# The first block's modulation vector made in two halves of the channels instead of whole

## The chip, the cores and the metric

The kernel runs on one core of one Trainium2 chip. The metric is the device time of one execution in microseconds (us). TensorE (PE in the profile) multiplies, with its weight loads listed apart as PEld; VectorE is DVE, ScalarE is ACT, GpSimd is POOL. SyncE (SP) issues nearly all transfers, and the issuing instructions of a queue stand in the profile as SPq or ACTq. All engines run their own instructions in a fixed order and wait for each other by semaphores.

## What is computed

256 tokens of width 1024 pass through two blocks. Only the head of the first one is touched:

```python
def first_block(x, c, ctx, c_ctx, w_ada, b_ada, norm1_g, w_in, ...):
    mod = silu(c) @ w_ada + b_ada                       # 6 x 1024: shift, scale, gate, shift, scale, gate
    sh_a, sc_a, gt_a, sh_m, sc_m, gt_m = split(mod, 6)
    mod_c = silu(c_ctx) @ w_ada + b_ada                 # the same for the context tokens
    csh_a, csc_a, ... = split(mod_c, 6)
    hc = rmsnorm(ctx, norm1_g) * (1 + csc_a) + csh_a
    s_f, s_b = context_states(hc, w_in, w_decay, b_decay)     # k, v and decay of the context
    h = rmsnorm(x, norm1_g) * (1 + sc_a) + sh_a
    x = x + gt_a * token_mixer(h, w_in, ..., s_f, s_b)        # gated linear attention, pool mixer, w_out
    x = x + gt_m * hier_moe(rmsnorm(x, norm2_g) * (1 + sc_m) + sh_m, ...)   # 32 experts, all run
    return rmsnorm(x, final_norm_g)
def reference(...):
    return second_block(first_block(...), ...)          # FFN, attention and retention, FFN, gate
```

So nothing can be multiplied by w_in before the shift and the scale (the first 2048 columns of `w_ada`, 8 MB) are there for the channels in question.

## The kernel before

Weights stream from memory through five buffers of 1 MB (`raw`), filled in turn by SP's queue; a load waits until the buffer's last reader is done, and all that stands behind it on SP waits with it. A large product is made in fp32r with a split: `split` writes the upper part `hi` of a weight piece on ACT (L197) and the rest `lo` on DVE (L198), and each K block (128 channels) takes three matmuls, hi by high part, hi by low part, lo by high part (L293 to L295). The order of instructions on the engines is set by a tile scheduler that goes by the code's order and the data's readiness; `after(...)` and the list `behind` push one instruction of an engine behind others, and `manual_schedule` keeps PE to the order of the code.

The head of the program runs as follows. The first 2048 columns of `w_ada` come as eight loads of 128 x 2048, one for each K block (three, then ctx and x, then five). The silu of c and c_ctx is made from a transposed copy of both vectors (L273, L277), and `ada_row` (L384) multiplies it with each of the eight blocks, four matmuls a block, into one bank. `ada_end` adds the bias (L390) and copies the row (L392); four transposes (L454) turn it, L456 to L460 make the scale (`gaT`), and L467 modulates the transposed and normalized tokens: first the eight blocks of the context `cT`, then the eight of `xT`. Each four blocks are split at once (L197, L198) into `cTh`/`cTl` and the parts of `xT2`. Meanwhile ctx and x are normalized (L426) and transposed (L432).

Then PE computes `aT` (L508, 32 matmuls, the low-rank decay input), the decay product (L521, four fp32 matmuls with `wd`), the panel `pq` (w_in columns 0 to 511: q and k, 48 matmuls of 256 columns for the context and 48 of 512 for x) and the panel `pv` (columns 512 to 1023, 96 matmuls of 512). ACT makes the log of the decay behind L521: Abs into `lt` (L522), a table load, Exp (L526), a table load, Ln (L529); DVE subtracts (L530) and the result is split into `lh`/`ll`. DVE also takes 24 partial products of later `w_ada` columns (`ada_step`, L405). Behind `pv` come the cumulated sums (L543), `ek` (L584, L585), the states (L592), the rest of the mixer, `w_out`, the router (L1039 and after) and the experts, whose first product is L1089. Expert weights come in pieces of 3 MB (`mw`, L703).

Of the kernel before, what the change touches and what calls it, by code (L numbers as in the profile page):

```python
# [81 lines left out]
def body(ctx: ExitStack, tc: tile.TileContext, I, out, dbg=None):  # L82
# [193 lines left out]
    G.memset(sT, 0.0)  # L276
    S.activation(sT[:, :, 0:2], vT[:, 0:16].rearrange("p (v k) -> p k v", v=2), AF.Silu)  # L277
    g1T = vT[:, 16:24]
    pscT = vT[:, 24:28]
    rgnT = vT[:, 28:36]  # L280

    def tok_mm(pa, lhs, w, c0, n, starts, stops, kh, skip=(0, 0)):

        raw = kxn(w, 4 * kh, 4, c0, n)
        for k2 in range(2):
            hi, lo = split(raw[:, 2 * k2:2 * k2 + 2, :])
# [99 lines left out]
    def ada_end(pa, j0, nch):  # L386

        for j in range(nch):
            sel = ident[:12, j0 + j:j0 + j + 1].to_broadcast([12, 32])
            mm(pa[32 * j:32 * j + 32, :], sel, b12, start=False, stop=True)  # L390
# [1314 lines left out]
```

## Time and profile before

| what | value |
|---|---|
| runs of before | 1088.04, 1092.1 and 1092.26 us, median 1092.1 |
| profiled execution | 1089.5 us, span 1087.2 |
| PE busy | 997.5 us (92% of the span), 5785 matmuls |
| PE weight loads | 741.5 us (68%) |
| DVE busy | 648.6 us (60%) |
| ACT busy | 493.5 us (45%) |
| POOL busy | 5.7 us (1%) |
| moved from memory | 258.54 MB, mean 240 GB/s over the span |
| mean granted clock of PE | 0.971 of full speed |

The table says where the engines are over the whole span. A change in the first 60 us is read from that stretch alone: what PE waits for there, and which queue is behind. The rows do that, in the section below.

### The profile page before, as it was taken

Reading aid. Unit: us, or ns where it says so; the run is one execution under the profiler, and the core shown is the slowest. Engines: PE = TensorE matmul, PEld = TensorE weight load, DVE = VectorE, ACT = ScalarE, POOL = GpSimd, SP = SyncE. Lnnn points to the kernel's source line nnn. Section 1 sums busy time; section 2 is a strip of 40 time slices with the busy share of each in tenths; the row PEclk is TensorE's granted clock in tenths of the full one; section 3 lists DMA queues with packets and bytes.
Section 4 is the critical chain, followed back from the end, with each engine's and each line's share of the span. In section 5 each row is a group of like instructions: output and inputs, shape, how many; then the busy total and the mean of one; then the engine's idle time right before and its main releaser. Section 6 shows DMA issues by size and latency. Waiting matters only on the chain.

```text
span 1087.2 us, 15196 instructions
## 1 busy us (share of the span) xinstructions
PE 997.5 (92%) x5785; PEld 741.5 (68%) x5786; DVE 648.6 (60%) x1260; ACT 493.5 (45%) x875; POOL 5.7 (1%) x14
## 2 busy tenths in 40 slices
PE   4799999898878787999999999999999999999996
PEld 1586776343333232888888876787888888888885
DVE  3893865332112124977674499858659677665466
ACT  3534354232112112655553354765565455554353
POOL 1000000000000000000000000000000000000000
PEclk9899998899889999899999999999999999999998
DMA  9786866799989999665555542354367366555511
GB/s 377 275 293 190 305 235 251 293 422 419 422 361 420 422 420 370 211 207 183 205 213 192 157 165 97 130 189 155 117 205 260 120 213 200 173 215 210 187 68 39
DMA packets 114658, 260.59 MB, mean 240 GB/s; under 512 B 7205, under 2 KB 73993, under 8 KB 101273
## 3 DMA queue, kind: packets, MB, share of 16 engines
q1 hardware_dynamic: 114096, 259.31, 65.4%
q8 instruction: 48, 0.79, 0.3%
q10 hardware_dynamic: 488, 0.28, 0.1%
q14 instruction: 26, 0.21, 0.0%
HBM read 258.54 MB, written 1.05 MB: 239 GB/s over the span
## 4 chain that ended last, share of the span: by engine, by line
PE 58%; DMA 6%; DVE 4%; ACT 2%; issue 1%; SPq 0%; DVEq 0%; ACTq 0%
PE mm L311 20%; PE mm L313 9%; PE acc L333 4%; PE acc L335 4%; PE acc L331 4%; DMA mw<-in_w_expert_out_dram 3%; DMA mw<-in_w_expert_in_dram 2%; PE mm L1089 2%; PE acc L1253 2%; PE acc L1252 2%; PE acc L1260 2%; PE acc L294 1%; PE acc L295 1%; PE acc L293 1%; DMA raw<-in_ffn_w_up_dram 1%
## 5 line engine op out<-in xcount | busy, mean ns | idle before, releaser
L198 DVE TENSOR_TENSOR lo<-raw,hi 128x1024 fp32r<-128x1024 f32 (+1 forms) x240 | 287.3, 1205 | 160.6 <-ACT hi L197 158.9
L197 ACT CAST hi<-raw 128x1024 fp32r<-128x1024 f32 (+1 forms) x240 | 246.8, 1036 | 221.1 <-PE mm L311 93.7
L311 PE MATMUL mm<-xT,hi 128*128 128x512 f32 x832 | 211.8, 396 | 0.6 <-DVE rs L1532 0.6
L311 PEld LDWEIGHTS mm<-xT,hi 128*128 128x128 f32 x832 | 148.5, 188 | 28.6 <-DVE rs L1532 1.0
L313 PEld LDWEIGHTS mm<-xT,lo 128*128 128x128 f32 x832 | 110.5, 188 | 9.4
L313 PE MATMUL mm<-xT,lo 128*128 128x256 f32 x832 | 112.1, 277 | 0.0
L1089 PE MATMUL mm<-mw,xg 128*32 (+1 forms) x704 | 85.8, 632 | 11.9 <-DMA mw<-in_w_expert_in_dram 10.9
L1089 PEld LDWEIGHTS mm<-mw,xg 128*32 128x32 f32 x704 | 22.2, 115 | 63.7 <-issue 52.4
L295 PE MATMUL acc<-lo,xT 128*128 128x512 f32 x144 | 57.1, 401 | 1.9 <-DVE lo L198 1.9
L293 PE MATMUL acc<-hi,xT 128*128 128x512 f32 x144 | 58.1, 404 | 0.0
L294 PE MATMUL acc<-hi,xT 128*128 128x512 f32 x144 | 57.7, 401 | 0.0
L335 PE MATMUL acc<-lo,hh 128*128 128x512 f32 x176 | 56.2, 393 | 0.0
L333 PE MATMUL acc<-hi,hl 128*128 128x512 f32 x176 | 56.0, 392 | 0.0
L331 PE MATMUL acc<-hi,hh 128*128 128x512 f32 x176 | 55.9, 392 | 0.0
L1053 ACT ACTIVATE xg<-mm,shT,gmT 128x256 f32<-128x256 f32 (+1 forms) x48 | 23.4, 545 | 67.8 <-PE mm L1039 67.8
L1111 PE MATMUL mm<-mw,z 128*32 128x512 f32 (+1 forms) x352 | 41.5, 601 | 5.5 <-DMA mw<-in_w_expert_out_dram 4.9
L1094 ACT ACTIVATE esg<-mm 128x256 f32<-128x256 f32 x11 | 4.2, 383 | 81.6 <-PE mm L1089 81.6
L1064 DVE TENSOR_TENSOR g<-mm,cst 128x8 f32<-128x8 f32 x11 | 1.8, 167 | 64.5 <-PE mm L1061 64.5
L1252 PE MATMUL acc<-hi,xT 128*128 128x256 f32 (+1 forms) x120 | 37.2, 334 | 2.3 <-ACT xT L197 2.3
L333 PEld LDWEIGHTS acc<-hi,hl 128*128 128x128 f32 x176 | 33.1, 188 | 7.4
L335 PEld LDWEIGHTS acc<-lo,hh 128*128 128x128 f32 x176 | 33.1, 188 | 7.3
L331 PEld LDWEIGHTS acc<-hi,hh 128*128 128x128 f32 x176 | 32.9, 188 | 7.5
(484 smaller groups left out, 1523.6 us busy)
## 6 DMA issues: line engine op xcount, KB each, us to landing
mw<-in_w_expert_in_dram SPq DMA_DIRECT2D x20, 3072.0 KB, 24.8
raw<-in_w_in_dram SPq DMA_DIRECT2D x32, 1024.0 KB, 5.0
mw<-in_w_expert_out_dram SPq DMA_DIRECT2D x10, 3072.0 KB, 26.1
raw<-in_w_ada_dram SPq DMA_DIRECT2D x24, 1024.0 KB, 7.8
raw<-in_ffn_w_gate_dram SPq DMA_DIRECT2D x22, 1024.0 KB, 6.7
raw<-in_ffn_w_up_dram SPq DMA_DIRECT2D x22, 1024.0 KB, 5.4
raw<-in_ffn_w_down_dram SPq DMA_DIRECT2D x22, 1024.0 KB, 5.0
raw<-in_w_out_dram SPq DMA_DIRECT2D x8, 1024.0 KB, 5.0
```

The costliest lines, as they stand in the source:

```text
L197: S.copy(hi, src)
L198: return V.tensor_tensor(lo, src, hi.bitcast(F32), op=ALU.subtract)
L293: mm(o, h_[k][:, c], hi[:, kk, z], start=k == starts, stop=False)
L294: mm(o, l_[k][:, c], hi[:, kk, z], start=False, stop=False)
L295: mm(o, h_[k][:, c], lo[:, kk, z], start=False, stop=k == stops)
L311: mm(pb, hi[:, k, :], x2[k], start=k == 0, stop=False, skip_group_check=True)
L313: mm(pb[:, 0:256], lo[:, k, :], x2[k][:, 0:256], start=False, stop=k == nk - 1, skip_group_check=True)
L331: mm(pa[t][n], hh[k][:, c], hi[:, 0, n * 512:(n + 1) * 512], start=k == seq[0], stop=False)
L333: mm(pa[t][n], hl[k][:, c], hi[:, 0, n * 512:(n + 1) * 512], start=False, stop=False)
L335: mm(pa[t][n], hh[k][:, c], lo[:, 0, n * 512:(n + 1) * 512], start=False, stop=k == seq[-1])
L1089: mm(st_["hp"][32 * i:32 * i + 32, :], xgs[q // 2][k // 4][:, k % 4, c:c + 32], w, start=k == 0, stop=k == KD - 1, skip_group_check=True)
L1252: mm(outs[i][t][:, c], xTh[:, k, tk], hi, start=k == 0, stop=False)
```

## The change

The modulation is made for channels 0 to 511 first and for 512 to 1023 behind it. `ada_half(b, k2)` loads, for half b, two K blocks of the shift's 512 columns and two of the scale's, as two transfers of 128 x 2 x 512 (512 KB with rows of 2 KB) into one `raw` buffer. The channels of c are dealt to partitions as (p k), so c and c_ctx are loaded as columns (`csil`) with no transpose ahead of the silu, and the bias row is loaded on ACT's queue. SP's order is now: one piece of half 0, ctx, one piece, x, two pieces, the first four K blocks of w_in, then all of half 1, then the other four K blocks of w_in.

Half 0 takes 16 matmuls and two for the bias; the row copy is followed by four small matmuls with a selector (`msel`) instead of four transposes. x is transposed behind the last matmul of half 0 (`after([last])`). Then DVE modulates four blocks of the context and four of x, and the panel `pq` starts on K blocks 0 to 3, in two pieces (`k2s`, `parts`). Between the pieces PE makes half 1's 18 matmuls, under `manual_schedule`; the second piece of the context covers the row copy, that of x the small matmuls' outcome. `wah` is split behind the second modulation, `aT` is next to K blocks 4 to 7 of `pq`, and the decay product (L569 now) stands behind the whole panel. `tri` is rounded on ACT (L560) instead of DVE.

```diff
-    nc.scalar.dma_start(vrow[0:8, :], I["c"][0].rearrange("(k p) -> k p", p=P))
-    nc.scalar.dma_start(vrow[8:16, :], I["c_ctx"].rearrange("(k p) -> k p", p=P))
+    csil = small(16, "csil", 1).rearrange("p (v k) -> p v k", v=2)
+    for v, name in enumerate((I["c"][0], I["c_ctx"])):
+        nc.scalar.dma_start(csil[:, v, :], name.rearrange("(p k) -> p k", k=KD))
...
+    G.memset(sT, 0.0)
+    S.activation(sT[:, :, 0:2], csil.rearrange("p v k -> p k v"), AF.Silu)
     ps = bank()
-    nc.tensor.transpose(ps[:, :36], vrow, ident[:36, :36])
-    V.tensor_copy(vT, ps[:, :36])
...
+    def tok_mm(pa, lhs, raw, n, starts, stops, kh, skip=(0, 0), k2s=(0, 1), parts=None):
+        for k2 in k2s:
+            hi, lo = parts or split(raw[:, 2 * k2:2 * k2 + 2, :])
...
-    w_ada0 = [kxn(I["w_ada"][0], k, 1, 0, 2048) for k in range(3)]
...
+    w_in = I["w_in"][0]
+    w_ada = I["w_ada"][0].rearrange("(p k) f -> p k f", k=KD)
...
+    def ada_half(b, k2):
+        w = weight("raw").rearrange("p (j k f) -> p j k f", j=2, k=2)
+        for j in range(2):
+            nc.sync.dma_start(w[:, j], w_ada[:, 2 * k2:2 * k2 + 2, D * j + 512 * b:D * j + 512 * b + 512])
+        return w
+    halves_a = [ada_half(0, 0)]
...
+    halves_a.append(ada_half(0, 1))
...
-    def ada_row(pa, w, k, nch):
-        for j in range(nch):
-            mm(pa[32 * j:32 * j + 32, :], sT[:, k, :], w[:, 512 * j:512 * j + 512], start=k == 0, stop=False)
...
+    halves_a += [ada_half(0, 2), ada_half(0, 3)]
+    first = kxn(w_in, 0, 4, 0, 512)
...
+    msel = small(4, "msel", 1).rearrange("p (j v) -> p j v", j=2)
+    pairs = ident.rearrange("p (e j v) -> p e j v", e=2, j=2)[:, :, :, 0:2]
+    V.tensor_tensor(msel, pairs[:, 0], pairs[:, 1], op=ALU.add)
...
+    def ada_part(pa, w, k2, b):
+        for j in range(2 if k2 == 3 else 0):
+            sel = ident[:12, 2 * j + b:2 * j + b + 1].to_broadcast([12, 32])
+            mm(pa[32 * j:32 * j + 32, :], sel, b12, start=False, stop=False, skip_group_check=True)
+        for kk in range(2):
+            for j in range(2):
+                i = 2 * kk + j
+                last = mm(pa[32 * i:32 * i + 32, :], sT[:, 2 * k2 + kk, :], w[:, j, kk, :], start=k2 == 0,
+                          stop=k2 == 3 and kk == 1, skip_group_check=True)
+        return last
...
+    def ada_row(pa):
         row = t2("modrow")
-        S.copy(row[:32 * nch, :], pa[:32 * nch, :])
-        return row
+        return row, S.copy(row, pa)
...
+    def ada_end(row, b):
+        pt = bank()
+        for s in range(4):
+            mm(pt[:, 4 * s:4 * s + 4], row[:, s * P:(s + 1) * P], msel.rearrange("p j v -> p (j v)"), start=True, stop=True)
+        V.tensor_copy(modT[b], pt[:, 0:16].rearrange("p (s j v) -> p s j v", s=4, j=2))
+        V.scalar_tensor_tensor(gaT[b], modT[b][:, :, 1, :], 1.0, g1T[:, 4 * b:4 * b + 4, None].to_broadcast([P, 4, 2]),
+                               op0=ALU.add, op1=ALU.mult)
...
-    cT, cTt = norm_T(cin, "cT")
-    xT, xTt = norm_T([xres[:, 0, :], xres[:, 1, :]], "xT")
-    pa = acc()
-    for k in range(KD):
-        w = w_ada0.pop(0) if w_ada0 else kxn(I["w_ada"][0], k, 1, 0, 2048)
-        ada_row(pa, w[:, 0, :], k, 4)
-    row = ada_end(pa, 0, 4)
...
+    cT, cTt = turned(normed(cin), "cT")
+    xn = normed([xres[:, 0, :], xres[:, 1, :]])
...
+    def modulate(b, v, src, tiles, hs, ls):
+        for s in range(4):
+            k = 4 * b + s
+            V.tensor_scalar(src[k], src[k], gaT[b][:, s, v:v + 1], modT[b][:, s, 0, v:v + 1], op0=ALU.mult, op1=ALU.add)
+        return split_act(hs[b], ls[b], tiles[b])
...
+    pa = bank()
+    for k2 in range(4):
+        last = ada_part(pa, halves_a[k2], k2, 0)
+    with after([last]):
+        xT, xTt = turned(xn, "xT")
+    row, copied = ada_row(pa)
+    ada_end(row, 0)
+    c_in = (1, cT, cTt, cTht, cTlt)
+    x_in = (0, xT, xTt, [xTh[:, 0:4, :], xTh[:, 4:8, :]], [xTl[:, 0:4, :], xTl[:, 4:8, :]])
+    behind[:] = [copied, modulate(0, *c_in)]
+    nc.sync.dma_start(wa, w_in[:, 1536:1568].rearrange("(k p) f -> p k f", p=P))
+    halves_b = [ada_half(1, k2) for k2 in range(4)]
+    first = [first, kxn(w_in, 4, 4, 0, 512)]
...
-    tri0 = weight("raw")[:, 0:640]
-    nc.sync.dma_start(tri0, I["cst"][:, 512:])
-    V.tensor_copy(tri, tri0)
-    pt = bank()
-    for s in range(4):
-        nc.tensor.transpose(pt[:, s * P:(s + 1) * P], row[:, s * P:(s + 1) * P], ident)
...
-    gaT = cp.tile([P, KD, 2], F32, name="gaT")
-    V.tensor_scalar(gaT, modT[:, 8:16, :], 1.0, None, op0=ALU.add)
-    V.tensor_tensor(gaT, gaT, g1T[:, :, None].to_broadcast([P, KD, 2]), op=ALU.mult)
...
+    pq = [(acc(), acc()), (acc(), acc())]
+    pa = bank()
+    parts = split(first[0][:, 0:2, :])
+    behind[:] = [modulate(0, *x_in)]
+    tok_mm(pq, (cL, xL), first[0], 512, 0, KD - 1, 0, (256, 0), (0,), parts)
+    parts = split(first[0][:, 2:4, :])
+    with tc.manual_schedule(engines={mybir.EngineType.PE}):
+        for k2 in range(4):
+            ada_part(pa, halves_b[k2], k2, 1)
+        row, copied = ada_row(pa)
+        tok_mm(pq[:1], (cL,), first[0], 512, 0, KD - 1, 0, (256,), (1,), parts)
+        ada_end(row, 1)
+        tok_mm(pq[1:], (xL,), first[0], 512, 0, KD - 1, 0, (0,), (1,), parts)
+    behind[:] = [copied, modulate(1, *c_in), modulate(1, *x_in)]
...
     wah = weight("hi", "wah")[:, :512].rearrange("p (k f) -> p k f", k=KD)
-    split_act(wah[:, :, 0:32], wah[:, :, 32:64], wa)
+    with after(behind):
+        split_act(wah[:, :, 0:32], wah[:, :, 32:64], wa)
+    behind[:] = []
...
+    tok_mm(pq, (cL, xL), first[1], 512, 0, KD - 1, 1, (256, 0))
+    tri0 = weight("raw")[:, 0:640]
+    nc.sync.dma_start(tri0, I["cst"][:, 512:])
+    S.copy(tri, tri0)
...
-    pq = tok_panel((cL, xL), w_in, 0, 512, (256, 0), ada_some)
+    ada_some()
+    ada_some()
```

Three places show what this does to the engines' orders. First PE, from the last `w_ada` matmuls on; `cTh`, `cTl` and `xT` are modulated tokens, `hi` a piece of w_in, `wah` the decay weights. Before:

```order
L384 MATMUL acc<-raw,sT 32x512 x12
L390 MATMUL acc<-b_124,cst 32x512 x4
L454 MATMUL mm<-cst,modrow 128x128 x4
L508 MATMUL mm<-cTh_325,wah 64x256
L508 MATMUL mm<-cTl_327,wah 32x256 x2
L508 MATMUL mm<-cTh_325,wah 64x256
```

and after:

```order
L402 MATMUL mm<-b_110,cst 32x512 x2
L406 MATMUL mm<-raw,sT 32x512 x4
L466 MATMUL mm<-cst,xn 128x128 x16
L421 MATMUL mm<-msel,modrow 128x4 x4
L406 MATMUL mm<-raw,sT 32x512
L295 MATMUL acc<-hi,cTh_246 128x256 x2
L406 MATMUL mm<-raw,sT 32x512 x3
L295 MATMUL acc<-hi,xT_115 128x512
L296 MATMUL acc<-hi,cTl_248 128x256 x2
L295 MATMUL acc<-hi,xT_115 128x512
L406 MATMUL mm<-raw,sT 32x512
```

The sixteen transposes of x stand between half 0's last matmul and the small ones, and the panel's first matmuls (L295) stand among half 1's L406.

Second PE where the decay product stands. Before, between `aT` and the first pieces of `pq`:

```order
L508 MATMUL mm<-xT_112,wah 64x256
L521 MATMUL mm<-wd,aTc 128x512 x2
L295 MATMUL acc<-lo,cTh_325 128x256
L508 MATMUL mm<-xT_112,wah 32x256
L508 MATMUL mm<-xT_112,wah 64x256
```

and after, at the end of `pq` (the 256-column matmuls are `pq`'s for the context, the 512-column ones with cTh are `pv`'s):

```order
L295 MATMUL acc<-hi,xT_115 128x512
L296 MATMUL acc<-hi,xT_115 128x512
L297 MATMUL acc<-lo,xT_115 128x512
L569 MATMUL mm<-wd,aTc 128x512 x2
L569 MATMUL mm<-wd,aTx 128x512 x2
L295 MATMUL acc<-hi,cTh_246 128x512
L296 MATMUL acc<-hi,cTl_248 128x512
```

The decay product has gone from the panel's start to its end, 24 matmuls of `pv` (K blocks 0 to 3 of the context) ahead of those that take the next piece of w_in.

Third ACT around the log of the decay. Before, `hi` behind the two Ln is a piece of `pv`, and `ck` is copied from the finished `pq`:

```order
L522 ACTIVATE lt<-mm 128x512
L526 ACT_TABLE_LOAD
L526 ACTIVATE lt<-lt 128x1024 x2
L529 ACT_TABLE_LOAD
L529 ACTIVATE lt<-lt 128x1024 x2
L197 CAST hi<-raw 128x1024
L197 CAST lh<-la 128x1024
L197 CAST hi<-raw 128x1024
L197 CAST lh<-la 128x1024
L562 COPY ck<-acc 128x256
```

and after:

```order
L611 COPY ck<-acc 128x256 x2
L197 CAST hi<-raw 128x1024
L570 ACTIVATE lt<-mm 128x512 x4
L574 ACT_TABLE_LOAD
L574 ACTIVATE lt<-lt 128x1024 x2
L577 ACT_TABLE_LOAD
L577 ACTIVATE lt<-lt 128x1024 x2
L197 CAST hi<-raw 128x1024
L197 CAST lh<-la 128x1024
```

The copies of `ck` have moved ahead of the log; the piece `hi` of w_in that the 25th matmul of `pv` takes stands behind it.

## Rows read from the trace of the kernel before

**Rows 1.** The page, busy tenths of PE in 40 slices of the span:
```profile
PE   4799999898878787999999999999999999999996
```

**Rows 2.** Windows, core 0: us, then busy (instructions) by engine, PEclk, DMA share, GB/s:
```profile
3.00:10.00 7.00, 0.29 (x1) 0.18 (x1) 0.68 (x4) 0.00 (x0) 0.00 (x0) 1.00 1.02 408
...
20.00:30.00 10.00, 9.37 (x56) 4.50 (x60) 7.25 (x24) 4.37 (x7) 1.02 (x2) 0.85 1.04 391
...
220.00:420.00 200.00, 164.53 (x1180) 70.35 (x1183) 46.36 (x92) 36.52 (x70) 0.00 (x0) 0.96 1.00 411
```

**Rows 3.** Timeline of PE: start, us, line, out<-in, xcount [idle before <-releaser]:
```profile
28.78 2.78 PE L384 MATMUL acc<-raw,sT 128*32 128x512 f32 x24
...
33.26 0.66 PE L454 MATMUL mm<-cst,modrow 128*128 128x128 f32 x4 [0.71 <-ACT modrow L392]
37.75 0.48 PE L508 MATMUL mm<-cTh,wah 128*64 128x256 f32 x1 [3.84 <-ACT cTh L197]
```

**Rows 4.** Timeline of ACT, the copied row and the first split of modulated tokens:
```profile
32.62 0.58 ACT L392 COPY modrow<-acc 128x512 f32<-128x512 f32 x1 [1.25 <-PE acc L390]
36.65 1.05 ACT L197 CAST cTh<-cT 128x1024 fp32r<-128x1024 f32 x1 [3.45 <-DVE cT L467]
```

**Rows 5.** Timeline of DVE, copies of the transposed x, then the first modulations:
```profile
27.91 2.48 DVE L434 COPY xT<-mm 128x512 f32<-128x512 f32 x4 [1.82 <-PE mm L432]
...
34.84 1.06 DVE L467 TENSOR_SCALAR cT<-cT,gaT,modT 128x256 f32<-128x256 f32 x3
35.81 0.49 DVE L451 CAST tri<-raw 128x640 fp32r<-128x640 f32 x1
```

**Rows 6.** Windows again, two stretches at the lower granted clock:
```profile
39.00:43.00 4.00, 3.90 (x19) 3.48 (x20) 4.00 (x11) 3.43 (x5) 0.00 (x0) 0.50 1.04 395
...
91.40:94.70 3.30, 3.30 (x28) 2.76 (x28) 0.00 (x0) 0.00 (x0) 0.00 (x0) 0.50 0.27 80
```

**Rows 7.** Timeline of PE, neighbours of 256 and of 512 columns; the last starts `pv`:
```profile
61.26 0.29 PE L294 MATMUL acc<-hi,cTl 128*128 128x256 f32 x1
61.38 0.28 PE L295 MATMUL acc<-lo,cTh 128*128 128x256 f32 x1
...
64.71 0.39 PE L295 MATMUL acc<-lo,xT 128*128 128x512 f32 x1
64.94 0.39 PE L293 MATMUL acc<-hi,cTh 128*128 128x512 f32 x1
```

**Rows 8.** Groups of PE by form, 37 to 65 us: line, out<-in xcount | busy us, mean ns:
```profile
L521 PE MATMUL mm<-wd,aTc 65*128 65x512 f32 x4 | 1.9, 592 | 0.0
```

**Rows 9.** Timeline of ACT, the log of the decay and the split behind it:
```profile
51.44 0.60 ACT L522 ACTIVATE lt<-mm 128x512 f32<-128x512 f32 x1
52.06 1.28 ACT L526 ACT_TABLE_LOAD   x1
53.35 2.01 ACT L526 ACTIVATE lt<-lt 128x1024 f32<-128x1024 f32 x2
55.38 1.28 ACT L529 ACT_TABLE_LOAD   x1
56.67 2.01 ACT L529 ACTIVATE lt<-lt 128x1024 f32<-128x1024 f32 x2
58.59 1.03 ACT L197 CAST hi<-raw 128x1024 fp32r<-128x1024 f32 x1
```

**Rows 10.** Timeline of DVE and of PE behind `pv`:
```profile
89.78 1.29 DVE L585 TENSOR_TENSOR ek<-ek,ck 128x512 f32<-128x512 f32 x2 [6.61 <-ACT ek L584]
...
90.53 0.43 PE L592 MATMUL mm<-cv,ek 128*64 128x128 f32 x2 [1.91 <-DVE ek L585]
```

**Rows 11.** Timeline of PE, a wait inside a later panel:
```profile
120.23 0.50 PE L295 MATMUL acc<-lo,xT 128*128 128x512 f32 x1 [1.91 <-DVE lo L198]
```

**Rows 12.** Waits of SP's queue, 0 to 210 us: line <- releaser: us, times, longest:
```profile
SPq L703 <- PE mm L1089: 22.0, 1, 22.0
```

**Rows 13.** The page, DMA packets by size:
```profile
DMA packets 114658, 260.59 MB, mean 240 GB/s; under 512 B 7205, under 2 KB 73993, under 8 KB 101273
```

More of the change, by code (lines that the diff above doesn't have):

```diff
@@ L268, in body @@
     CI = cp.tile([P, 2, 32], F32R, name="CI")
-    vT = cp.tile([P, 36], F32, name="vT")
+    vT = cp.tile([P, 20], F32, name="vT")
     sT = cp.tile([P, KD, 32], F32, name="sT")
+    G.memset(sT, 0.0)
+    S.activation(sT[:, :, 0:2], csil.rearrange("p v k -> p k v"), AF.Silu)
     ps = bank()
-    nc.tensor.transpose(ps[:, :36], vrow, ident[:36, :36])
-    V.tensor_copy(vT, ps[:, :36])
+    nc.tensor.transpose(ps[:, :20], vrow, ident[:20, :20])
+    V.tensor_copy(vT, ps[:, :20])
     V.tensor_copy(cstr, cst[:, 0:3, :])
     V.tensor_copy(CI, v2(cst[:, 3, 0:64]))
[L276 to L286, printed above, removed]
+    g1T = vT[:, 0:8]
+    pscT = vT[:, 8:12]
+    rgnT = vT[:, 12:20]
+    def tok_mm(pa, lhs, raw, n, starts, stops, kh, skip=(0, 0), k2s=(0, 1), parts=None):
+        for k2 in k2s:
+            hi, lo = parts or split(raw[:, 2 * k2:2 * k2 + 2, :])
             for s, (h_, l_) in enumerate(lhs):
@@ L299, in tok_panel @@
         for kh in range(2):
-            tok_mm(pa, lhs, w, c0, n, 0, KD - 1, kh, skip)
+            tok_mm(pa, lhs, kxn(w, 4 * kh, 4, c0, n), n, 0, KD - 1, kh, skip)
             if between:
@@ L379, in body @@
         nc.sync.dma_start(cin[t], I["ctx"][0, t * P:(t + 1) * P, :])
+    halves_a.append(ada_half(0, 1))
+    for t in range(2):
         nc.sync.dma_start(xres[:, t, :], I["x"][0, t * P:(t + 1) * P, :])
-    def ada_row(pa, w, k, nch):
-        for j in range(nch):
-            mm(pa[32 * j:32 * j + 32, :], sT[:, k, :], w[:, 512 * j:512 * j + 512], start=k == 0, stop=False)
[L386 to L390, printed above, removed]
-        row = t2("modrow")
-        S.copy(row[:32 * nch, :], pa[:32 * nch, :])
-        return row
+    halves_a += [ada_half(0, 2), ada_half(0, 3)]
[13 more added lines that the diff above has]
+        return last
+    gaT = [cp.tile([P, 4, 2], F32, name=f"gaT{b}") for b in range(2)]
+    modT = [cp.tile([P, 4, 2, 2], F32, name=f"modT{b}") for b in range(2)]
+    def ada_row(pa):
+        row = t2("modrow")
+        return row, S.copy(row, pa)
[6 more added lines that the diff above has]
+                               op0=ALU.add, op1=ALU.mult)
     def ada_wide(j):
@@ L402, in ada_step @@
     def ada_step(part, j, k2):
-        w = load(I["w_ada"][0, 2 * k2 * P:(2 * k2 + 2) * P, j * D:(j + 1) * D].rearrange("(k p) f -> p k f", p=P), 2, D)
+        w = load(w_ada[:, 2 * k2:2 * k2 + 2, j * D:(j + 1) * D], 2, D)
         for kk in range(2):
@@ L426, in norm_T, with turned @@
             S.activation(xn[t], src[t], AF.Copy, scale=rr[t])
+        return xn
+    def turned(xn, name):
+        dst, tiles = blocks(name, KD)
         for k2 in range(4):
@@ L435, in norm_T @@
         return dst, tiles
-    cT, cTt = norm_T(cin, "cT")
-    xT, xTt = norm_T([xres[:, 0, :], xres[:, 1, :]], "xT")
-    pa = acc()
-    for k in range(KD):
-        w = w_ada0.pop(0) if w_ada0 else kxn(I["w_ada"][0], k, 1, 0, 2048)
-        ada_row(pa, w[:, 0, :], k, 4)
-    row = ada_end(pa, 0, 4)
-    nc.sync.dma_start(wa, I["w_in"][0][:, 1536:1568].rearrange("(k p) f -> p k f", p=P))
+    cT, cTt = turned(normed(cin), "cT")
+    xn = normed([xres[:, 0, :], xres[:, 1, :]])
+    cTh, cTht = blocks("cTh", KD, F32R)
+    cTl, cTlt = blocks("cTl", KD, F32R)
+    cL, xL = (cTh, cTl), (xTh_, xTl_)
+    def modulate(b, v, src, tiles, hs, ls):
[16 more added lines that the diff above has]
+    first = [first, kxn(w_in, 4, 4, 0, 512)]
     for i in range(2):
@@ L480, in gate_load @@
     def gate_load():
-        return [kxn(I["w_ada"][0], 4 * (k2 % 2) + 2 * (k2 // 2), 2, 5 * D, D) for k2 in range(4)]
+        return [load(w_ada[:, k:k + 2, 5 * D:6 * D], 2, D) for k in (0, 4, 2, 6)]
     grow = cp.tile([P, 512], F32, name="grow")
```

32 lines of the change are left out of this document (7 added, 25 removed).

## The prediction

> **What bounds the kernel now.** The page comes first [rows 1]: PE is busy nine tenths or more in most slices, and the first two slices, of 27 us each, are the lowest of all (4 and 7). The windows say why [rows 2]: from 3 to 30 us the transfers run at 408 and 391 GB/s, all that this kernel ever gets (the experts' stretch shows 411), while PE is nearly empty to 10 us. The start is bound by bytes. PE's timeline shows the end of that phase [rows 3]: the last `w_ada` matmuls run to 28.78 + 2.78 = 31.6 us, and the first matmul with a modulated token starts at 37.75, its last wait being 3.84 us for ACT's split of `cTh`. Those 6.2 us are a chain on three engines [rows 3 to 5]: bias, row copy (0.58), transposes (0.66), scale, modulations, split (1.05). From the third slice on PE is full [rows 1], so whatever makes the panels start sooner moves all of PE's work. Whether the end follows is read from SP's waits [rows 12]: the expert stream, which runs at the full rate to 420 us [rows 2], waits 22.0 us for the first expert's matmuls. It starts when PE gets there, so a microsecond saved on PE in the first block is worth about one at the end.
>
> **Half 0 is there sooner.** Half of `w_ada`'s 8.39 MB, 4.19 MB, now lies behind it; at 408 GB/s [rows 2] that is 10.3 us, and half 0's last matmul ends at 31.6 - 10.3 = 21.3. The tail gains and loses. The bias matmuls no longer end it and `tri` (0.49 on DVE, between two modulations) is gone from it [rows 5]. But x's 16 transposes and their four copies now stand in it: the first bank 0.4, the copies 2.48 [rows 5], so 24.2. From the start of the old transposes to the first modulation took 34.84 - 33.26 = 1.6, of which 0.66 were PE's [rows 3, 5]: 0.9 more, 25.1. Four modulations are 1.06 x 4/3 = 1.4 and the split 1.05 [rows 4, 5]: 27.6. I take 28, since x has to be normalized by then. **The panel starts 37.75 - 28 = 9.7 us sooner.**
>
> **What the panel costs more.** Half 1's 18 matmuls, 0.23 each by the spacing of 512-column neighbours [rows 7], 4.1 us, stood in front, where PE waited for bytes anyway; now they are inside the panel and on PE's path. Half 1 itself is not late: 4.19 MB and 1.18 MB of w_in behind half 0's landing at 20.4 take 13.2 us, to 33.6; PE gets to its last matmuls at 28 + 24 panel matmuls (12 x 0.12 + 12 x 0.23 = 4.2) + 14 of half 1 (3.2) + about 1 at the lower clock = 36.4. So the loads have 2.8 us to spare, which is the cover; beyond it every microsecond counts. Half 1's own tail (copy, small matmuls, four modulations, split: 0.6 + 0.9 + 1.4 + 1.05 and the x part behind it on DVE) is covered by the second piece, 12 x 0.12 + 12 x 0.23 = 4.2 us, not wholly: I take 2.5 us of waits. The lower clock: in 39 to 43 us PE ran at 0.50, 1.2 GHz, behind its 3.84 us wait [rows 3, 6]; the same comes at 28, 0.8 us. The stretch from the first modulated matmul to the end of `pq` was 64.94 - 37.75 = 27.2 us. Its work at full clock is 80 matmuls at 0.12 and 48 at 0.23 and the decay product, 2 x 1.9 [rows 7, 8]: 9.6 + 11.0 + 3.8 = 24.4, so 2.8 were waits and lower clock. After: 24.4 + 4.1 + 2.5 + 0.8 = 31.8, from 28 to 59.8. **`pq` ends 5.1 us sooner**, with 3.5 and 6.5 as ends (1 to 4 us of waits, 0 to 1.5 of lower clock).
>
> **A new wait.** The decay product moves from the panel's start to its end, and ACT's log of the decay with it. Before, the chain from the last `lt` to the split of `pv`'s next piece ran from 51.44 to 58.59 + 1.03 = 59.6 [rows 9], 8.2 us under `pq`'s matmuls. After, it starts when L569 ends, and PE has only the 24 matmuls of `pv` that need no new piece: 24 x 0.23 = 5.5 us [rows 7]. The next matmul needs `hi`, which ACT makes behind both Ln. **PE waits 8.2 - 5.5 = 2.7 us**, and `pv`'s other 72 matmuls wait with it, x's of the first pieces among them. The waits of 1.91 us at 90.5 and what followed it, 3.3 us at 0.50 [rows 6, 10], show what may come behind: up to 3.3 us at half speed cost 1.7; between 0 and that I take 0.8. So `pv` ends 5.1 - 2.7 - 0.8 = 1.6 us sooner.
>
> **Behind it.** DVE had 6.61 us free ahead of `ek` [rows 10]; its queue of `ada_step` now starts later against PE, by 2 to 4 us, which this cover takes. The pool panel's first 12 matmuls, which filled the stretch around 100 us, come later; there they fall on the wait of 1.91 us at 120.2 [rows 11]. Between nothing and 1.9 I take 0.9 as gain. The bias load on ACT's queue and the silu without a transpose end before any matmul needs them: nothing, and if that cover went, the small ones' cost is the first `w_ada` matmul's delay, at a time when PE has free time. SP's second w_in load waits for DVE's `lo` of the fourth piece of the first; all of SP's later loads stand behind it. By my times it lands at 37 and is needed at 38.7.
>
> **The sum.** 1.6 + 0.9 = 2.5 us, passed on one for one: the profiled execution's 1089.5 becomes **1087.0**. The median of the runs is 2.6 above the profiled one; beside it the same saving would read 1089.6. About 0.5%, 5.4 us, is what a measurement of this kernel can tell from no change.
>
> **A rule against it.** The trace moves at 391 to 408 GB/s while transfers of 1 MB and of 512 KB (ctx, x) mix [rows 2], and its densest stretch, at 411, falls in an execution where 73,993 of 114,658 packets are under 2 KB [rows 13]. The Trainium skill, "DMA: Bandwidth & Descriptors", section Bandwidth, says to batch transfers to 1 MiB or more, and fits one alone at 2.0 us plus its bytes at 436 GB/s, so that (an estimate from that page) sixteen of 512 KB would take 51 us one after another, where eight of 1 MB took 35. By that rule the change would lose some 16 us at its start; by the rows, where loads queue behind each other at the full rate, it loses nothing.
>
> **The rivals.**
> *The new wait is hidden or small* (0.30). The 2.7 and the 0.8 are worked out from one order of ACT and PE; if L569's first three results let ACT begin, or `pv`'s 24 matmuls start late anyway, the 5.1 us come through, and with the whole 1.9 of [rows 11] 7.0: 1082.5. For it: three of the four `lt` can run while the fourth product is made. Against: Exp is ordered behind the last `lt`.
> *The loads are slower in halves* (0.12). Place: half 1's pieces, 512 KB with rows of 2 KB, before 34 us. The first 11.7 MB (`w_ada`, ctx, x, w_in) take 28.7 us at 408 GB/s, and each tenth off that rate costs 2.9 us. The first 2.8 are covered, the next 2.5 eat the saving: at 344 GB/s (5.3 us late) the result is nil, below 297 (10.7 late) it is slower by more than 0.5%; at 270, 14.7 us late, 1089.5 + 14.7 - 5.3 = 1098.9. For it: the window of 20 to 30 us is already at 391. Against: [rows 13]. The page's rule above would be this case.
> *The halves do not overlap* (0.10): the change does not do what it says. PE's order puts a matmul of half 1 ahead of the panel's first; if half 1's first piece or x's normalization came as late as 37, PE would start where it started before, with 4.1 us more to do but less waiting: within 2 us of nothing, 1089.5.
> *The stream swallows it* (0.08). If the experts' transfers, and not PE, set their own start, the saving vanishes: 1089.5. [Rows 12] speak against it.
>
> **How the numbers follow.** The forecast, 1 to 5 us saved, has 0.40. Faster by over 0.5% is the first rival and a little of the forecast's upper end: 0.33. Slower by over 0.5% is the second rival's worse part and a bad start in the third: 0.13. The rest, 0.54, is within 0.5%. For the range I go down past 1082.5 with the end of the panel's term (6.5 instead of 5.1), to 1081 and, as the first rival is not rare, a microsecond and a half further, 1079.5; and up to the point where slow loads have cost the saving and 4.5 us more, 1094.
>
> **What would show it.** In the profile after: half 0's last matmul near 21 us and the first L295 near 28 (if 33 or later: the third rival); half 1's last matmul not waiting for a transfer (else the second); the first `pv` matmul near 59.8 instead of 64.94; then one PE wait of 2 to 3 us for ACT's `hi`, some 24 matmuls into `pv`, with Ln ahead of it on ACT; the granted clock behind it; `ek` some 1.6 us sooner; and the first L1089 2 to 4 us sooner. If L1089 is sooner and the end is not, the passing on is what I had wrong.

## The result

The changed kernel takes **1102.7 us** (median, 1101.9 to 1105.1), the kernel before 1090.9 us in the same set of runs: ratio 1.0118, with a 95% interval of 1.0097 to 1.0138. It is 1.2% slower, where 1087.0 was predicted, and outside the range. The profiled execution has a span of 1099.9 us against 1087.2.

The page of the kernel after; the tenths answer [rows 1]:

```profile
span 1099.9 us, 15233 instructions
...
PE   4888999797888687999999999999999999999997
...
DMA packets 118113, 260.59 MB, mean 237 GB/s; under 512 B 7604, under 2 KB 74376, under 8 KB 105752
```

Nothing new stands out there: 92% of the span is PE's, as before. The place of the loss is read from points that both traces have (us from the span's start, from the timelines):

| point | before | after | difference |
|---|---|---|---|
| first product with a modulated token | 37.75 | 29.59 | -8.2 |
| first product of `pv` | 64.94 | 64.91 | 0.0 |
| last copy of v ends | 87.84 | 93.71 | +5.9 |
| pool mixer's panel ends | 124.99 | 128.88 | +3.9 |
| first product of the experts | 199.53 | 203.92 | +4.4 |
| second block: last low-part product of the FFN's first panel ends | 452.73 | 457.39 | +4.7 |
| end of the span | 1087.2 | 1099.9 | +12.7 |

Two losses, then. The panel starts 8.2 us sooner, `pv` starts no sooner and ends later. And 8.0 us are lost between 457 us and the end, in the second block, where the change has not moved, added or taken away one instruction. ("Second block" with a time stands below for the stretch from the sixth point of the table to the end: 634.5 us before, 642.5 after.)

**The first loss.** PE's timeline of the kernel after (start, us, line, xcount, [idle before <-releaser]; each fp32 product of 32 rows has two records) answers [rows 3, 7]:

```profile
22.84 1.97 PE L466 MATMUL mm<-cst,xn 128*128 128x128 f32 x16
...
26.95 1.14 PE L406 MATMUL mm<-raw,sT 128*32 128x512 f32 x2 [1.35 <-DMA raw<-in_w_ada_dram]
29.59 0.80 PE L295 MATMUL acc<-hi,cTh 128*128 128x256 f32 x2 [1.50 <-ACT cTh L197]
...
33.76 1.42 PE L406 MATMUL mm<-raw,sT 128*32 128x512 f32 x2
...
41.41 1.07 PE L406 MATMUL mm<-raw,sT 128*32 128x512 f32 x8
42.41 0.39 PE L295 MATMUL acc<-hi,cTh 128*128 128x256 f32 x1
...
64.91 0.80 PE L295 MATMUL acc<-hi,cTh 128*128 128x512 f32 x1
...
73.74 0.50 PE L295 MATMUL acc<-hi,cTh 128*128 128x512 f32 x1 [2.66 <-ACT hi L197]
```

Half 1's last product ends at 42.4, where 37.3 followed from the prediction (36.4 and the 0.9 of the last four); and 24 products into `pv` stands the 2.66 us wait. The windows (columns as in [rows 2]) and DVE's timeline show what PE was doing meanwhile:

```profile
3.00:10.00 7.00, 0.26 (x1) 0.18 (x1) 1.06 (x7) 2.84 (x6) 0.00 (x0) 1.00 0.95 336
20.00:30.00 10.00, 7.15 (x44) 3.65 (x40) 6.40 (x19) 5.91 (x7) 0.52 (x1) 0.89 1.07 365
26.00:29.00 3.00, 1.14 (x2) 0.14 (x2) 2.74 (x11) 1.23 (x2) 0.25 (x1) 0.79 1.06 386
29.00:32.00 3.00, 2.41 (x8) 0.70 (x8) 3.00 (x6) 1.59 (x2) 0.00 (x0) 0.50 1.05 387
32.00:35.00 3.00, 3.00 (x9) 1.24 (x6) 2.29 (x3) 0.00 (x0) 0.00 (x0) 0.58 1.00 365
```

```profile
29.66 1.23 DVE L198 TENSOR_TENSOR cTl<-cT,cTh 128x1024 fp32r<-128x1024 f32 x1
30.80 1.22 DVE L198 TENSOR_TENSOR lo<-raw,hi 128x1024 fp32r<-128x1024 f32 x1
31.93 1.23 DVE L198 TENSOR_TENSOR xT<-xT,xT 128x1024 fp32r<-128x1024 f32 x1
33.07 1.23 DVE L198 TENSOR_TENSOR lo<-raw,hi 128x1024 fp32r<-128x1024 f32 x1
44.91 0.17 DVE L422 COPY modT<-mm 128x16 f32<-128x16 f32 x1 [10.61 <-PE mm L421]
```

From 29 to 35 us PE's clock is at or near its lower level (0.50 and 0.58 of 2.4 GHz), behind the three microseconds from 26 to 29 in which PE was busy 1.14. DVE is busy for 5.3 of the same six microseconds, until 34.3, with the four splits that the first piece's products take one after another. The two columns together are the reading: PE counts as busy, at half speed, and takes its pieces as DVE hands them over. Then DVE has nothing for 10.61 us, as half 1's end is late.

**The second loss.** PE's timeline in the second block's FFN, a stretch of equal groups of eight 512-column and eight 256-column products, before and then after:

```profile
505.76 2.02 PE L311 MATMUL mm<-xT,hi 128*128 128x512 f32 x8
507.63 1.07 PE L313 MATMUL mm<-xT,lo 128*128 128x256 f32 x8
508.54 2.02 PE L311 MATMUL mm<-xT,hi 128*128 128x512 f32 x8
```

```profile
508.55 2.03 PE L313 MATMUL mm<-xT,hi 128*128 128x512 f32 x8
510.42 1.12 PE L315 MATMUL mm<-xT,lo 128*128 128x256 f32 x8
511.38 2.03 PE L313 MATMUL mm<-xT,hi 128*128 128x512 f32 x8
```

From group to group it is 1.87 + 0.91 us before and 1.87 + 0.96 after, with no wait in either. The eight products of 256 columns, same shapes, same clock, take 50 ns longer. The page counts 832 of each kind, 104 such pairs: by the means over two long stretches (1.864 + 0.911 and 1.870 + 0.961) that is 104 x 0.056 = 5.8 of the 8.0 us; most other products of the block are slower too, by about 1% (512 columns of `acc<-hi,xT` take 407 ns instead of 402), and PE's waits in it are not longer than before. What has changed for them is one thing only, which the diff does not show as such: `vT` shrank by 64 bytes in each partition and `csil` and `msel` are new, so what is allocated behind them lies elsewhere in on-chip memory. By the addresses in the two built programs, the second block's weight buffers `raw`, `hi` and `lo` lie 96 bytes further from the token tiles (`xres`, `xT2`) than before, and from the working tiles that are allocated between the two.

### The profile page after: what moved, and what is told of

Its sections match the earlier page's. It is cut to its first block, busy times and chain, and to the rows that moved or that the text cites. A ratio compares the mean times of both kernels' runs of the same rounds, so it can differ in the third digit from the quotient of the medians.

```text
span 1099.9 us, 15233 instructions
## 1 busy us (share of the span) xinstructions
PE 1011.7 (92%) x5797; PEld 750.1 (68%) x5798; DVE 648.3 (59%) x1261; ACT 495.4 (45%) x877; POOL 5.7 (1%) x14
## 4 chain that ended last, share of the span: by engine, by line
PE 59%; DMA 6%; DVE 4%; ACT 2%; issue 1%; SPq 0%; DVEq 0%; ACTq 0%
PE mm L313 20%; PE mm L315 10%; PE acc L333 5%; PE acc L335 5%; PE acc L337 4%; DMA mw<-in_w_expert_out_dram 2%; DMA mw<-in_w_expert_in_dram 2%; PE mm L1138 2%; PE acc L1302 2%; PE acc L1301 2%; PE acc L1309 2%; PE acc L296 1%; PE acc L297 1%; PE acc L295 1%; DMA raw<-in_ffn_w_up_dram 1%; ACT hi L197 1%
## 5 line engine op out<-in xcount | busy, mean ns | idle before, releaser
L315 PEld LDWEIGHTS mm<-xT,lo 128*128 128x128 f32 x832 | 114.0, 188 | 9.3
L315 PE MATMUL mm<-xT,lo 128*128 128x256 f32 x832 | 116.9, 283 | 0.0
L1138 PE MATMUL mm<-mw,xg 128*32 (+1 forms) x704 | 85.8, 632 | 12.1 <-DMA mw<-in_w_expert_in_dram 11.2
L295 PE MATMUL acc<-hi,xT 128*128 128x512 f32 x144 | 58.9, 410 | 0.7 <-ACT xT L197 0.7
L1301 PE MATMUL acc<-hi,xT 128*128 128x256 f32 (+1 forms) x120 | 37.6, 337 | 2.2 <-ACT xT L197 2.2
L1302 PE MATMUL acc<-hi,xT 128*128 128x256 f32 (+1 forms) x120 | 37.1, 337 | 1.2 <-DVE xT L198 1.2
```

The costliest lines, as they stand in the source:

```text
L295: mm(o, h_[k][:, c], hi[:, kk, z], start=k == starts, stop=False)
L315: mm(pb[:, 0:256], lo[:, k, :], x2[k][:, 0:256], start=False, stop=k == nk - 1, skip_group_check=True)
L1138: mm(st_["hp"][32 * i:32 * i + 32, :], xgs[q // 2][k // 4][:, k % 4, c:c + 32], w, start=k == 0, stop=k == KD - 1, skip_group_check=True)
L1301: mm(outs[i][t][:, c], xTh[:, k, tk], hi, start=k == 0, stop=False)
```

## Experiments on the place of the buffers

Six kernels add padding to a small tile, or take it away, and move no instruction. A distance is given as the bytes by which token tiles and weight buffers lie further apart than in before. First the kernel after with `msel` 32 bytes longer, which makes 128 bytes:

```diff
-    msel = small(4, "msel", 1).rearrange("p (j v) -> p j v", j=2)
+    msel = small(12, "msel", 1)[:, 0:4].rearrange("p (j v) -> p j v", j=2)
```

> The changed kernel with its selector tile msel padded by 32 bytes; no instruction differs, only where the buffers behind it lie in on-chip memory: the weight buffers raw, hi and lo are back at 32 bytes past a multiple of 64, as in the kernel before (the change put them on a multiple of 64). Theory (place of the buffers): the 8 us that the changed kernel loses behind the experts come from its 256-column matmuls, 0.96 us for eight instead of 0.91, because of where lo lies; then eight take 0.91 again and the time is about 1102.7 - 8 = 1094.7. Rival (something else that the change moved in the second block, such as the order of banks or buffers): nothing changes, 1102.7.

Measured: 1097.1 us (1094.2 to 1099.7), ratio to before 1.0058 [1.0039, 1.0078]: 5.6 us better than after, where the theory had 8. The second block gives the whole 8.0 and takes 634.5 us again; but in e1's profile the experts (first product to the sixth point of the table) take 256.6 us, and 253.5 in after's. That stretch is no matter of the distance: it is 253.2 in before and 256.5 in e10, 253.8 in e4 and 256.4 in e3, pairs at the same distance. Then the kernel before with `gsel`, which lies between the two, 32 bytes longer:

```diff
-    gsel = small(2, "gsel", 1)
+    gsel = small(10, "gsel", 1)[:, 0:2]
```

> The kernel before with its selector tile gsel padded by 32 bytes, no instruction differs: its weight buffers move onto a multiple of 64 bytes, where the change put them. Theory (place of the buffers): eight 256-column matmuls of the second block go from 0.91 to 0.96 us and the time from 1090.9 to about 1099. Rival: 1090.9, nothing changes.

Measured: 1100.8 us, ratio 1.0082 [1.006, 1.0103]; second block 641.1. The kernel before loses most of what after lost, with no change of its work; of the 9.8 us the second block shows 6.6. I then took the rule to be the buffers' own address modulo 64 bytes, and tried 64 bytes (`small(18, ...)` in the same line), and 32 bytes for tokens and weights together:

> Before, with gsel made 64 bytes longer instead of the 32 of e2; all the small tiles and weight buffers behind it lie 64 bytes later, at the same remainder by 64 as in before, and no instruction is added or moved. Theory 1 (the place of the weight buffers modulo 64 bytes sets the pace of the matmuls): the time is before's, 1091, the second block from the FFN's first panel to the end 634.5 as before. Theory 2 (any distance from before's layout costs, or the distance between token tiles and weights): slower by about as much as e2, 1098 to 1101, the second block 641.

Measured: 1099.5 us, ratio 1.0081 [1.0053, 1.011]; second block 641.2. The theory of the address modulo 64 fell.

```diff
-    vT = cp.tile([P, 36], F32, name="vT")
+    vT = cp.tile([P, 44], F32, name="vT")
```

> Before, with the first small tile (vT) 32 bytes longer, so that the token tiles (xres, xT2) and the weight buffers all lie 32 bytes later; in e2 the weight buffers alone did. No instruction is added or moved. Theory 1 (the remainder of the weight buffers' own place by 64 bytes sets the pace): slow as e2, 1099 to 1101, second block 641. Theory 2 (what counts is where weights lie against the token tiles): before's time, 1091, second block 634.5.

Measured: 1091.8 us, ratio 1.0007 [0.9987, 1.0027]; second block 634.8. Moving both together by 32 bytes costs nothing: it is the distance that counts, not the place as such. Last, 128 bytes on before (`small(34, ...)`), and the best kernel of the next section without its padding:

> Before, with gsel made 128 bytes longer; all behind it lies 128 bytes later against the token tiles. No instruction is added or moved. So far: 0 (before, e10) and 128 bytes more (e1, e4, e6, e8) between token tiles and weight buffers gave a second block of 634 to 635 us; 32 (e2), 64 (e7) and 96 (after) gave 641 to 642.5. Theory 1 (the distance counts modulo 128 bytes): the second block 634.5, the time before's 1091. Theory 2 (before's layout is a single good one, and the after variants with padding are good for a reason of their own): second block 640 or more, 1098 to 1101.

Measured: 1093.3 us, ratio 1.0021 [1.0004, 1.0039]; second block 634.7. The first theory holds for the second block, whose pace is that of e1, not that of before; by the pace, 128 bytes are not a full period. Of the 1.7 us over the 1091.6 of before in this set the second block shows 0.2; the rest I cannot place.

```diff
-    msel = small(12, "msel", 1)[:, 0:4].rearrange("p (j v) -> p j v", j=2)
+    msel = small(4, "msel", 1).rearrange("p (j v) -> p j v", j=2)
```

> The kernel of e11 without the 32 bytes of padding in msel: the weight buffers lie as in after. Theory 1 (the place costs its own 6 to 8 us, whatever the first block does): 6 to 8 us over e11, the second block 641 to 643 instead of 634.5. Theory 2 (the place and the late first block are one effect): within 2 us of e11.

Measured: 1097.1 us, 7.8 over e11; second block 642.7. The place costs its own 8 us, whatever the first block does.

The layouts side by side, the pace as the mean time from a group of eight to the next, over 455 to 620 and 870 to 1000 us:

| distance, bytes | kernel | 8 of 512 columns, us | 8 of 256 columns, us | second block, us |
|---|---|---|---|---|
| 0 | before | 1.864 | 0.911 | 634.5 |
| 0 | e10 | 1.865 | 0.913 | 634.8 |
| 32 | e2 | 1.874 | 0.937 | 641.1 |
| 64 | e7 | 1.865 | 0.948 | 641.2 |
| 96 | after | 1.870 | 0.961 | 642.5 |
| 96 | e13 | 1.867 | 0.962 | 642.7 |
| 128 | e1 | 1.835 | 0.927 | 634.5 |
| 128 | e12 | 1.835 | 0.926 | 634.7 |

The groups of PE by form from 480 to 560 us say the same in one row each (mean ns of one 256-column product at the end): before, e2, e7, after.

```profile
L313 PE MATMUL mm<-xT,lo 128*128 128x256 f32 x232 | 31.2, 277 | 0.0
```

```profile
L313 PE MATMUL mm<-xT,lo 128*128 128x256 f32 x232 | 31.9, 279 | 0.0
```

```profile
L313 PE MATMUL mm<-xT,lo 128*128 128x256 f32 x232 | 32.2, 281 | 0.0
```

```profile
L315 PE MATMUL mm<-xT,lo 128*128 128x256 f32 x228 | 32.0, 282 | 0.0
```

So the second loss is shown, from both kernels and in both directions. Not shown is what in the chip makes it: whether PE's two reads meet, or PE and the engines that write the next split. Nor is the pair of tiles singled out: the padding moves the weight buffers against the working tiles as well as against the tokens.

## Experiments on the first block

All five build on the padded kernel e1, so that they can be compared with before. The first makes half 1's 18 products together behind the panel's first piece, instead of among it, as they looked scattered at the lower clock:

```diff
-                        mm(o, h_[k][:, c], lo[:, kk, z], start=False, stop=k == stops)
+                        last = mm(o, h_[k][:, c], lo[:, kk, z], start=False, stop=k == stops)
+        return last
...
-    tok_mm(pq, (cL, xL), first[0], 512, 0, KD - 1, 0, (256, 0), (0,), parts)
+    piece = tok_mm(pq, (cL, xL), first[0], 512, 0, KD - 1, 0, (256, 0), (0,), parts)
...
-        for k2 in range(4):
-            ada_part(pa, halves_b[k2], k2, 1)
+        with after([piece]):
+            for k2 in range(4):
+                ada_part(pa, halves_b[k2], k2, 1)
```

> The padded changed kernel (e1), with half 1's 18 matmuls together behind the first piece of pq instead of scattered in it. Theory (a scattered matmul of 32 rows costs 0.9 to 1.4 us where four in a row, one for each quarter of the array, share that time): the 18 cost PE about 4 us instead of 8, and half 1's last matmul ends some 2 to 3 us sooner than at 42.4; time 2 to 3 us under e1. Rival (the lateness is the lower clock and late loads): it ends within 1 us of 42.4 and the time is that of e1.

Measured: 1097.6 us, ratio 1.0057 [1.0036, 1.0079], as e1; half 1's last product ends at 41.9, 0.6 sooner than in after. PE's timeline:

```profile
37.12 2.78 PE L407 MATMUL mm<-raw,sT 128*32 128x512 f32 x24
39.84 1.05 PE L403 MATMUL mm<-b,cst 12*32 12x512 f32 x4
40.81 1.06 PE L407 MATMUL mm<-raw,sT 128*32 128x512 f32 x8
```

The first piece alone, with nothing between, lasts until 37.1. It is the piece itself that is slow; the theory that the mixing costs fell.

The second writes the log of the decay (Exp, Ln, subtraction, split) behind `pv` in the code, so that ACT's `hi` no longer stands behind it:

> The padded changed kernel (e1), with Exp, Ln and the split of the decay's log written behind the panel pv, so that ACT splits pv's next pieces of w_in ahead of them. Theory (the wait of 2.66 us in pv and the 1.6 us of lower clock behind it are all on PE's path): pv ends 4 us sooner than in e1, and the time is 3 to 4 us under e1. Rival (what pv gains is given back before the experts, since ek then waits for the log): within 1 us of e1.

```diff
-    for i in range(2):
-        with after([last]):
-            last = S.activation(lt[i], lt[i], AF.Exp, scale=-1.0)
...
     pv = tok_panel((cL, xL), w_in, 512, 512, (0, 0), ada_some)
...
         S.copy(v_[:, t, :], pv[1][t])
+    for i in range(2):
+        with after([last]):
+            last = S.activation(lt[i], lt[i], AF.Exp, scale=-1.0)
...
```

Measured: 1092.3 us (1088.1 to 1096.3), ratio 1.0003 [0.9985, 1.0021]: 4.8 us less than e1. The wait of 2.66 us is gone and v's last copy ends at 88.61 instead of 92.18. Behind `pv` a new wait of 1.2 us appears, for `ll`; the one for `ek`, 2.1 in e1, is 1.2:

```profile
PE mm L641 <- DVE ek L634: 1.2, 1, 1.2
PE mm L576 <- DVE ll L198: 1.2, 1, 1.2
```

In the two profiles most of the 3.6 us is given back before the experts, as the rival had it: their first product starts at 203.05, in e1 at 203.91. Another 2.7 us lie in the experts' stretch (256.6 in e1, 253.8 here), which varies. So the medians, whose intervals lie apart, agree with the theory, and the profiles show 0.9 us of it; how much of the 4.8 us is the wait's is not shown.

Then, on top of e4, two kernels for the slow first piece. One fills PE's empty time, behind half 0's small products (`last`), with products that nobody reads; the other transposes x behind the context's fourth modulation. The first:

```diff
+    idle = bank()
+    with after([last]):
+        for i in range(6):
+            mm(idle[:, 0:256], ident, cst[:, 0:2, :].rearrange("p a b -> p (a b)"), start=True, stop=True, skip_group_check=True)
```

> The kernel of e4 (after, with 32 bytes of padding and the log behind pv), and six extra products of 256 columns on PE behind the small msel matmuls; nobody reads their result, and their cost is part of the time. In e4 PE is half empty from 26 to 32 us (1.5 of 3 busy in each window), and the granted clock is 0.83 from 29 to 32 and 0.60 from 32 to 35; the last of half 1's matmuls ends at 42.6. Theory 1 (the lower clock behind PE's wait is what makes half 1 late): the clock stays at 1.00, the first piece is 2 to 3 us shorter, half 1's last matmul ends near 40, pv and what is behind it come 2 us sooner than in e4, time 1090. Theory 2 (DVE's splits and modulations set the first piece, 3.00 of 3 busy from 29 to 35): half 1's last matmul within 0.7 us of 42.6, time as e4's 1092, whatever the clock.

Windows of e4, then of e6:

```profile
29.00:32.00 3.00, 1.49 (x8) 0.49 (x8) 3.00 (x8) 2.09 (x2) 0.00 (x0) 0.83 1.05 385
32.00:35.00 3.00, 3.00 (x12) 1.19 (x6) 3.00 (x3) 0.00 (x0) 0.00 (x0) 0.60 1.02 373
```

```profile
29.00:32.00 3.00, 2.68 (x12) 0.79 (x11) 3.00 (x7) 2.09 (x2) 0.00 (x0) 1.00 1.04 379
32.00:35.00 3.00, 3.00 (x17) 1.84 (x15) 2.89 (x3) 0.00 (x0) 0.00 (x0) 1.00 0.98 365
```

Measured: 1090.4 us, ratio 0.9986 [0.9969, 1.0003]. The clock stays at 1.00, half 1's last product ends at 40.8 instead of 42.6, `pv` starts at 63.1 instead of 65.0: the first theory, and 1.9 us for the lower clock at this point. The medians are the same 1.9 us apart, but their intervals overlap, so that the gain in the whole time is not shown.

The other (`scaled[-1]` is the context's fourth modulation):

```diff
-    with after([last]):
-        xT, xTt = turned(xn, "xT")
     row, copied = ada_row(pa)
-    ada_end(row, 0)
+    last = ada_end(row, 0)
...
+    first_c = modulate(0, *c_in)
+    with after([last, scaled[-1]]):
+        xT, xTt = turned(xn, "xT")
```

> The kernel of e4, with x's transposes and their four copies placed behind the context's four modulations instead of ahead of them: in e4 the copies take 2.48 us of DVE between half 0's last matmul and the first modulation, and the first modulated matmul starts at 30.5. Theory 1 (the tail of half 0 is the chain on DVE): the first modulated matmul starts at 28 to 28.5, x's part is at most 1 us later, half 1's last matmul comes 1.5 to 2 us sooner, and the time is 1.5 us under e4's, 1090.5. Theory 2 (the first piece is bound by the DVE work as a whole, in whichever order): the first matmul is sooner, but half 1's last matmul still ends within 0.7 us of 42.6, time 1092.

Measured: 1090.2 us, ratio 1.0001 [0.9984, 1.0018]. The panel's first product is at 29.37 instead of 30.51, but half 1's last one ends at 43.0, later than e4's 42.6, and `pv` starts at 66.9. The second theory, for the part that the trace shows. The median lies 2 us under e4's all the same, while the two intervals overlap; this profile gains those microseconds from 128 to 195 us, a stretch that varies (last section). I draw nothing from it.

The last one is e6 with the log written ahead of the copies of v, not behind them:

> The kernel of e6 (after, 32 bytes of padding, log behind pv, the extra products that keep PE busy), with the log of the decay and its split written ahead of the copies of v instead of behind them. In e6 ACT is idle from 73.8 to 81.9 us and makes the two lh only at 85.2 and 86.6, behind the copies of v, and DVE makes ll behind 9.2 us of ada_step; PE waits 1.17 for ll, 0.23 for lh and 1.24 for ek, and ek starts at 89.93. Theory 1 (these waits are the last of what the moved log costs): they go, ek starts near 88.5 and the time is 1 to 2 us under e6's, 1088.5 to 1089.5, under before's 1090.9. Theory 2 (the ada_step that DVE makes later takes its place, at ek or in the pool panel): ek is sooner, but the time is e6's, 1090.4.

```diff
     pv = tok_panel((cL, xL), w_in, 512, 512, (0, 0), ada_some)
+    for i in range(2):
+        with after([last]):
+            last = S.activation(lt[i], lt[i], AF.Exp, scale=-1.0)
...
     cv = v2(t4("cv"))
```

Measured: **1089.3 us** (1087.5 to 1091.3), before 1091.6, ratio 0.9981 [0.9968, 0.9994]. `ek` starts at 88.74 instead of 89.93. This is the version that beats both kernels, before by 0.2%. Against e6 it is 1.1 us less, with intervals that overlap, so its two theories stay undecided. Of e6's three waits for `ll`, `lh` and `ek`, 2.6 us together, the one for `ek` is left, and it is longer:

```profile
PE mm L645 <- DVE ek L638: 2.1, 1, 2.1
```

## Why the prediction was wrong

The prediction had the saving at 2.5 us on the profiled execution; 12.7 were lost, a miss of 15.2. Step by step:

| step | predicted, us | measured, us | adds to the miss |
|---|---|---|---|
| half 0's last product ends | 21.3 | 22.9 | in the next |
| panel's first product | 28 | 29.6 | 1.6 |
| from there to half 1's last product | 9.3 | 12.8 | 3.5 |
| from there to the first product of `pv` | 22.5 | 22.5 | 0 |
| `pv` takes longer by | 3.5 | 5.9 | 2.4 |
| taken up behind `pv` | 0.9 | 2.0 | -1.1 |
| pool mixer to the second block | 0 | 0.8 | 0.8 |
| second block | 0 | 8.0 | 8.0 |

**The step that failed most is not in the sum at all.** The price of the edits of `vT`, `csil` and `msel` was put at nothing, as small work with cover: "The bias load on ACT's queue and the silu without a transpose end before any matmul needs them: nothing". PE's work did not grow by them. As sizes of tiles they moved the second block's weight buffers by 96 bytes against the tokens, and that is 8.0 of the 15.2 us. No rival had it, and the rival that ended slower (slow loads) did not happen in the form in which it was priced.

**Half 0.** The 10.3 us for half the bytes were right in size; the start was not. From 3 to 10 us 336 GB/s were moved instead of 408 ([rows 2]): 72 GB/s over 7 us are 0.5 MB, 1.2 us at 408. Most of that is missing from 7 to 9 us, where 176 GB/s are moved, and 384 before. SP's queue has two waits at ctx's two loads, behind 1 and 1.5 MB of issued transfers, where 3 MB stood ahead of ctx before:

```profile
SPq L385 <- DMA cst<-in_cst_dram: 3.0, 1, 3.0
SPq L385 <- DMA csil<-in_c_dram: 1.8, 1, 1.8
```

So `csil`, put at nothing, has a part in this too; no run takes these waits away. The tail behind half 0 then took 6.7 us (22.9 to 29.6), just as the prediction has it.

**The first piece and half 1** was the worst term of the first block. The loads were not late: their last products waited for no transfer, as predicted, and the 1.35 us at 26.95 stand in a stretch in which PE would have waited for `cTh` anyway. "The lower clock: ... the same comes at 28, 0.8 us" had the mechanism and the place right, and the size wrong: with the clock held the stretch takes 10.6 us (e6, 30.2 to 40.8), in e4, which lacks nothing but the six added products, 12.1, and here 12.8: 1.5 to 2.2. The rest, 10.6 against the 8.3 that the sum had without clock, I put down to DVE's four splits (29.66 to 34.3), which the sum had no term for; the rows agree, no run takes them away.

**Half 1's tail.** 2.5 us of waits were allowed; the trace has 0.7 and 0.5. That the stretch to `pv` came out at 22.5 all the same is luck: PE's products took the 1.3 us more that the waits took less, although the decay product, 3.8 in the sum, took 3.0 (61.88 to 64.91).

**The new wait** was right in its mechanism and to a tenth: 2.7 predicted, 2.66 measured, at the 25th product of `pv`, with Ln ahead of `hi` on ACT. The tenth is partly luck: the last `lt` starts at 65.51, 0.6 behind `pv`'s first product, and the 24 products take 6.2 us instead of 5.5. Lower clock behind it, taken as 0.8 between 0 and 1.7: PE is at 0.57 from 75 to 79 us, about 1.7. In e1, with the same wait, the clock stayed at 1.00 there and v's last copy ended 1.5 sooner. Wait and clock make 4.4 of the 5.9 us by which `pv` is longer; the other 1.5 no run takes apart.

**Behind it.** "Between nothing and 1.9 I take 0.9": the wait of [rows 11] went wholly; 2.0 us were taken up to the pool mixer's end. And the passing on was right: SP's queue still waits for the experts' first products, by the same 22.0 us as in [rows 12]:

```profile
SPq L752 <- PE mm L1138: 22.0, 1, 22.0
```

**The rule on batching.** Half 1's transfers of 512 KB moved at 386 and 387 GB/s, in the windows above, the 1 MB loads before at 391 [rows 2]. Queued behind each other they lost some 1%. The Trainium skill, "DMA: Bandwidth & Descriptors", section Bandwidth, advises 1 MiB or more, on figures of loads that GpSimd issues; here SP issues them, and the trace does not show the cost.

## What to carry over

A change of a small tile's size is a change of every address behind it: where the matmuls bound the kernel, compare first the pace of a stretch that the edit left alone, and repeat the edit with padding before anything is concluded about the edit itself. An earlier start of PE is worth what the engines that feed it allow next; of 8.2 us of lead nothing was left 35 us later, as half 1's products (4.1 us) had come onto PE's path and its first work came in drops, at half clock. And when an engine's chain is moved, look for what its queue holds up behind it: that wait, priced from two rows, came out.

## What the runs showed of the hardware

**The place of the weight buffers against the token tiles changes the pace of matmuls.** 32, 64 or 96 bytes more between the two cost the second block 6.6 to 8.2 us of 634.5; 128 bytes more cost nothing in sum and gave a third pace, 1.835 us for eight products of 512 columns and 0.927 for eight of 256, where before had 1.864 and 0.911. The Trainium skill, "SBUF — State Buffer", section "SBUF: two separate sides", says that on the engine side only the port pair of VectorE and GpSimd causes contention, and that PE never waits on anyone. By that alone the layouts would be equal; the measurement differs, and which accesses meet is not shown.

**The lower clock does not follow every wait.** Behind the same 2.66 us wait it fell in after (0.57 from 75 to 79) and not in e1 (1.00 from 75 to 80). In the router's stretch, PE's timeline of before and of e6, behind a wait of 2.0 us in both:

```profile
184.16 2.06 PE L853 MATMUL mm<-grow,gsel 128*128 128x512 f32 x2
186.01 1.77 PE L831 MATMUL mm<-wr,x1T 128*128 128x40 f32 x8
187.57 2.05 PE L853 MATMUL mm<-grow,gsel 128*128 128x512 f32 x2
```

```profile
182.53 1.10 PE L907 MATMUL mm<-grow,gsel 128*128 128x512 f32 x2
183.47 0.98 PE L885 MATMUL mm<-wr,x1T 128*128 128x40 f32 x8
184.28 1.10 PE L907 MATMUL mm<-grow,gsel 128*128 128x512 f32 x2
```

The same products run at half speed in one profile (granted clock 0.59 and 0.50 from 183 to 189 us) and at full speed in the other (1.00 from 183 to 186). From the pool mixer's panel to the first product of L1039 (L1093 in e6, L1088 in e4) it took 69.3 us in before, 70.5 in e4 and 67.7 in e6, and the experts' stretch varies by 3.4: single profiles differ by more than most effects of the first block, so totals were taken from medians and the profile used for places alone.
